# A planned attention order with waits, holds and 72 tries, and split weights at other addresses

## The chip, the cores and the metric

The kernel runs on one NeuronCore of one Trainium2 chip. TensorE (PE) does the matrix products and has a second row in the profile for the loading of its weights (PEld); VectorE (DVE), ScalarE (ACT) and GpSimd (POOL) do the elementwise work, and SyncE (SP) issues most transfers. SBUF has 128 partitions, which every engine addresses by bytes within a partition; PSUM has eight banks of 128 x 512 fp32. The metric is the device time of one execution in microseconds, as the median of several.

## The reference, cut to what matters

The input is 512 tokens of width 1024. There are two layers, all in fp32:

```python
for layer in range(2):
    sh1, sc1, g1, sh2, sc2, g2 = split(silu(c) @ ada_w[layer] + ada_b[layer], 6)
    u = rms_norm(h, norm_g[layer, 0]) * (1 + sc1) + sh1
    y = hgrn2_mixer(u, ...) if layer == 0 else dilated_attention_mixer(u, ...)
    h = h + (1 + g1) * rms_norm(y, norm_g[layer, 1])
    u = rms_norm(h, norm_g[layer, 2]) * (1 + sc2) + sh2
    gate, up = split(u @ ffn_w_in[layer], 2)          # 1024 -> 2 x 2816
    y = (silu(gate) * up) @ ffn_w_out[layer]          # 2816 -> 1024
    h = h + (1 + g2) * rms_norm(y, norm_g[layer, 3])
```

The attention mixer makes queries, keys and values for three groups of heads, eight heads of 128 each, with windows and dilations (128, 1), (512, 4) and (2048, 16). It rotates the first 32 channels of queries and keys, takes a softmax within each group's window, and weighs the three groups' outputs by a softmax over their log sums.

## The kernel before, in words

**Products.** An fp32 product is done as three passes of a faster type (fp32r): a number is cut into a high part (ACT copies it, `hi`) and the rest (DVE subtracts, `lo`), and `hi*hi + hi*lo + lo*hi` is summed in PSUM. Larger products are also done by a scheme with seven block products in place of eight; its blocks are 256 columns wide, so a seven-product unit has 7 x 12 = 84 matmuls of 256 columns.

**Weights.** `Stream` holds all weight loads in one list, `items`. Each is loaded by SP into one of two buffers `raw` (1 MB, tag "raw", `bufs=2`), in the order of the list. When an item has been worked off, its buffer takes the next load. Kinds of items: a weight (`"w"`) is cut into `hi` and `lo` (L89 and L90); a weight for seven products (`"quarters"`, `"half"`) is summed and cut by the stage itself; `"ada"` is 1 MB of `ada_w`, worked off by four DVE operations of 128 x 512 (L390 and L392, in attention L1931 and L1933), of which two items make one half of a modulation vector, summed over the partitions by POOL (`partition_all_reduce`, L394 and L1936); `"rows"` are two loads of 256 KB that finish half a gate (L439 and L440) after that sum; `"do"` finishes a shift or scale and loads nothing. `hi` and `lo` lie in a ring of three tiles of 2048 + 128 elements, that is 8704 bytes a partition, and `places(i, first)` takes 2048 elements of it from element `first` on. `first` is `R0` = 16 in the FFN, `V0[...]` for the four units of attention's values, `Q0[head]` for queries and keys. One element is 4 bytes.

**Where the modulation items lie.** `weave` puts them between the weights. In FFN 0, the first half of the weights (`f0a`) has three plain pairs of weights and then 16 quarters; the second half (`f0b`) has 11 weights of `ffn_w_out`. The gate of that layer (0, 5) needs four `ada` items (`gate_loads`) and two `rows` items (`gate_fins`); before, half of them lie among the plain weights of `f0a` and the rest in `f0b`, in front of the eight `ada` items of the next layer's shift and scale (`rest`). A group of `f0b` is placed after every 0.8 weights.

**The seven products of the FFN** (`seven_products`, PE's line is L958) work through 16 units in FFN 0 and 18 in FFN 1. A unit has three products that use the weight's own parts R (of `places(i)[0]`, cut by L921 and L925) and four that use its sums. POOL adds once per unit (L929), which gives a unit's period in the trace.

**Attention.** `Plan` gets the tasks of the attention stage with an engine, a cost and what they read and write. `run` gives each a due time, backwards from the place that a PE task has in the order of the program (`goal`), and then plays the engines forward: a free engine takes the ready task that is due first; the engines' programs are written out in that order, and each engine works in order. A task that follows on another engine is ready `late` after its predecessor's end (0.55 us after PE, 0.3 after a DMA, 0.08 otherwise, and 2.2 after the small transfers of POOL), on the same engine at once. An engine is left idle only for a task marked `urgent` that is about to be ready. `ticks` spreads a head's steps over the units of the following heads: scores at its begin + 3, 5 and 7 ticks, `merged` (the softmax over the groups) at + 9, the transposes of the probabilities (`flipped`, PE's line is L2313) at + 10 and + 11, the sums over values at + 11 and + 12. The last head's steps fall into the output projection (L577 to L579 there), which ticks seven times more. PE's line for the products of queries, keys and values is L1974. Attention's `ada` items lie in the plan too, with four POOL sums.

Of the kernel before, what the change touches and what calls it, by code (L numbers as in the profile page):

```python
# [2 lines left out]

# [7 lines left out]
F32 = mybir.dt.float32  # L11
# [5 lines left out]
P = 128  # L17
S = 512
D = 1024
# [16 lines left out]
R0, V0, Q0 = 16, (112, 96, 64, 16), (16, 16, 16, 16, 48, 80, 112, 0)  # L36
# [103 lines left out]
class Plan:  # L140


    LATE = {"PE": 0.55, "DMA": 0.3}

# [3 lines left out]
    def add(self, eng, cost, fn=None, r=(), w=(), goal=None, late=None, urgent=False, other=None):  # L148

        t = dict(id=len(self.tasks), eng=eng, cost=cost, fn=fn, goal=goal, urgent=urgent, other=other,  # L150
                 late=self.LATE.get(eng, 0.08) if late is None else late, deps=set(), outs=[])
# [33 lines left out]

    def run(self):

        ts = self.tasks
        for t in ts:
            for d in t["deps"]:  # L190
                ts[d]["outs"].append(t["id"])
        for t in reversed(ts):
            due = min([ts[o]["due"] - t["late"] for o in t["outs"]], default=1e9)
            if t["goal"] is not None:
                due = min(due, t["goal"] + t["cost"])
            t["due"] = due - t["cost"]
        left = {t["id"]: len(t["deps"]) for t in ts}
        ready, free, wait, done, now = {}, {}, {}, [], 0.0
        events = []

        def finish(t, at):
            for o in t["outs"]:
                u = ts[o]
                late = 0.0 if u["eng"] == t["eng"] else t["late"]
                ready[o] = max(ready.get(o, 0.0), at + late)
                left[o] -= 1
                if not left[o]:
                    enter(u)
                    heapq.heappush(events, ready[o])

        def enter(t):
            wait.setdefault(t["eng"], []).append(t["id"])
            if t["other"]:
                wait.setdefault(t["other"][0], []).append(t["id"])

        for t in ts:
            if not left[t["id"]]:
                ready[t["id"]] = 0.0
                enter(t)
        heapq.heappush(events, 0.0)  # L220
        while events:
            now = heapq.heappop(events)
            moved = True
            while moved:
                moved = False
                for eng in list(wait):
                    able = [i for i in wait[eng] if ready[i] <= now + 1e-9]
                    if not able or free.get(eng, 0.0) > now + 1e-9:
                        continue
                    able.sort(key=lambda i: (ts[i]["due"], i))  # L230
                    for i in able:
                        soon = [u for u in wait[eng] if now + 1e-9 < ready[u] < now + ts[i]["cost"] - 0.15 and ts[u]["urgent"]
                                and ts[u]["due"] < ts[i]["due"] + 3.0]
                        if eng is None or not soon or ts[i]["urgent"]:
                            break
                    else:
                        continue
                    t = ts[i]
                    wait[t["eng"]].remove(i)
                    if t["other"]:  # L240
                        wait[t["other"][0]].remove(i)
                        if eng != t["eng"]:
                            t["eng"], t["cost"] = t["other"]
                    t["start"] = now
# [4 lines left out]
                    finish(t, now + t["cost"])  # L249
                    moved = True  # L250
        assert len(done) == len(ts)
        for t in done:
            if t["fn"]:
                t["fn"](t["eng"])
        return done
# [36 lines left out]
def block_kernel(tc, x, c, positions, ada_w, ada_b, norm_g, hgrn_w_in, lower, hgrn_norm_g, hgrn_w_out,  # L292
# [8 lines left out]
    with ExitStack() as ctx:  # L301
# [580 lines left out]
        def seven_products(fs, mid, seeded, spare, th, tl):  # L882
# [34 lines left out]

            def r_hi(i):
                if i < len(fs):
                    raw[i] = st.whole()  # L920
                    act.copy(places(i)[0][0][:, 0:1536], raw[i][:, 512:])  # L921

            def r_lo(i):
                hi, lo = places(i)[0]
                dve.tensor_sub(lo[:, 0:1536], raw[i][:, 512:], hi[:, 0:1536].bitcast(F32))  # L925
# [43 lines left out]
            with tc.manual_schedule(engines=ORDERED):  # L969
# [950 lines left out]
        def condition(item):  # L1920
# [19 lines left out]
            if kind == "do":  # L1940
                col = ("col", (l, v, hf))
                for k in range(4):
                    c = l * 4 + v - (1 if v > 2 else 0)
                    DVE(0.36, lambda k=k: to_col(cols[:, c, hf * 4 + k:hf * 4 + k + 1], a.t, k), [a()], [col + (k,)])
# [7 lines left out]
            DVE(0.65, lambda: dve.tensor_add(half_of(), a.t, raw.t[:, 0:512]), [a(), raw()], [place(hf)])  # L1952
            DVE(0.7, lambda: dve.scalar_tensor_tensor(half_of(), half_of(), 1.0, raw.t[:, 512:D], op0=OP.add, op1=OP.mult),
# [29 lines left out]
        def turned(g, rows, q, k, last=False):  # L1983
# [3 lines left out]
            DVE(0.37, lambda: dve.stream_shuffle(rot.t, rows.t, [(i + 16) % 32 for i in range(32)]), [rows(i) for i in range(4)], [rot()])  # L1987
            DVE(0.36, lambda: dve.tensor_mul(rot.t, rot.t, cs[:, 1]), w=[rot()])
            DVE(0.36, lambda: dve.tensor_mul(rows.t, rows.t, cs[:, 0]), w=[rows(i) for i in range(4)])
            DVE(0.36, lambda: dve.tensor_add(rows.t, rows.t, rot.t), [rot()], [rows(i) for i in range(4)])  # L1990
# [7 lines left out]
            for i, t in enumerate((q, k)):  # L1998
                for hf in range(2):
# [6 lines left out]
                    ACT(0.38 if g else 0.62, back_to, [rows(2 * i + hf)], [t(hf)] if g else [t(0), t(1)])  # L2006
# [8 lines left out]
        def sevens(g, hd):  # L2015
            s_ = {}

            def cut(part, k):
                raw, p = s_["raw"], s_["p1"]
                ACT(0.58, lambda: act.copy(Q(p.t[0], part), Q(raw.t, k)), [raw(k)], [p("h", part)])  # L2020
                DVE(0.62, lambda: dve.tensor_sub(Q(p.t[1], part), Q(raw.t, k), Q(p.t[0], part).bitcast(F32)), [raw(k), p("h", part)], [p("l", part)])

            def add(to, k):
                raw = s_["raw"]
                DVE(0.62, lambda: dve.tensor_add(Q(raw.t, to), Q(raw.t, to), Q(raw.t, k)), [raw(k)], [raw(to)])
# [13 lines left out]
            def prepare_2():  # L2039
                raw = s_["raw"]  # L2040
                s_["p2"] = p = split_place(Q0[hd])
                for n in (1, 0):
                    two = slice(n * 1024, n * 1024 + 1024)
                    keys = [2 * n, 2 * n + 1]
                    ACT(1.0, lambda two=two: act.copy(p.t[0][:, two], raw.t[:, two]), [raw(k) for k in keys], [p("h", k) for k in keys])
                    DVE(1.15, lambda two=two: dve.tensor_sub(p.t[1][:, two], raw.t[:, two], p.t[0][:, two].bitcast(F32)),  # L2046
# [446 lines left out]
```

## Time and profile before

| | us |
|---|---|
| median of 3 runs | 1519.95 (1515.9 to 1520.64) |
| the profiled execution | 1517.82 |
| its span | 1516.1 |
| PE busy | 1487.4 (98%) |
| PEld busy | 1329.4 (88%) |
| DVE busy | 1100.0 (73%) |
| ACT busy | 797.3 (53%) |
| POOL busy | 199.9 (13%) |

Busy times are sums over the span, and matmuls overlap in them. Five stretches of the program matter below: FFN 0 with its seven products (from about 381 to 529 us of the span), its second half (to about 650), attention and its output projection (about 707 to 1155), FFN 1 with its seven products (from about 1201 to 1390), and its second half. PEclk is the share of full clock that PE was granted; it is 1 but for stretches of 3.4 us at 0.5. A row of the view by windows has, after the stretch and its length, each engine's busy time with its number of instructions, PEclk, the DMA engines' busy share and GB/s.

### The profile page before, as it was taken

Reading aid. Unit: us, or ns where it says so; the run is one execution under the profiler, and the core shown is the slowest. Engines: PE = TensorE matmul, PEld = TensorE weight load, DVE = VectorE, ACT = ScalarE, POOL = GpSimd, SP = SyncE. Lnnn points to the kernel's source line nnn. Section 1 sums busy time; section 2 is a strip of 40 time slices with the busy share of each in tenths; the row PEclk is TensorE's granted clock in tenths of the full one; section 3 lists DMA queues with packets and bytes.
Section 4 is the critical chain, followed back from the end, with each engine's and each line's share of the span. In section 5 each row is a group of like instructions: output and inputs, shape, how many; then the busy total and the mean of one; then the engine's idle time right before and its main releaser. Section 6 shows DMA issues by size and latency. Waiting matters only on the chain. (4 is left out here: it accounts for less than half of the span.)

```text
span 1516.1 us, 25045 instructions
## 1 busy us (share of the span) xinstructions
PE 1487.4 (98%) x9807; PEld 1329.4 (88%) x9807; DVE 1100.0 (73%) x1812; ACT 797.3 (53%) x1470; POOL 199.9 (13%) x174
## 2 busy tenths in 40 slices
PE   8999999999999999999999999999999999999998
PEld 6777888888999987888999989998978899999886
DVE  4587867587788776677888786778666967777633
ACT  4443434362555533375647787377875555555231
POOL 1011211031111101140001010001012211110100
PEclk9999999999999999999999999999999999999999
DMA  9654444225333356623254342434353323334531
GB/s 308 185 162 144 151 137 167 84 84 178 102 112 110 112 174 222 223 108 118 84 166 124 105 120 83 142 84 132 94 150 107 112 85 112 112 112 139 193 113 56
DMA packets 210151, 201.09 MB, mean 133 GB/s; under 512 B 8248, under 2 KB 167920, under 8 KB 209776
## 3 DMA queue, kind: packets, MB, share of 16 engines
q1 hardware_dynamic: 207056, 192.71, 40.8%
q10 hardware_dynamic: 1952, 6.65, 1.3%
q8 instruction: 77, 1.26, 0.3%
q0 software_dynamic: 1024, 0.13, 0.2%
q14 instruction: 42, 0.34, 0.1%
HBM read 192.31 MB, written 5.31 MB: 130 GB/s over the span
## 5 line engine op out<-in xcount | busy, mean ns | idle before, releaser
L89 ACT CAST hi<-raw 128x2048 fp32r<-128x2048 f32 x43 | 82.1, 1910 | 148.2 <-DMA raw<-in_ffn_w_out_dram 63.6
L90 DVE TENSOR_TENSOR lo<-raw,hi 128x2048 fp32r<-128x2048 f32 x43 | 102.8, 2392 | 60.7 <-ACT hi L89 60.6
L577 PE MATMUL ps_mm<-uh,hi 128*128 128x512 f32 (+1 forms) x400 | 145.8, 364 | 0.0
L578 PE MATMUL ps_mm<-ul,hi 128*128 128x512 f32 (+1 forms) x400 | 143.7, 359 | 1.1 <-DVE ul L677 1.1
L1974 PE MATMUL ps_mm<-apart,hiq 128*128 128x256 f32 (+1 forms) x608 | 144.7, 330 | 0.0
L579 PE MATMUL ps_mm<-uh,lo 128*128 128x512 f32 (+1 forms) x400 | 144.1, 360 | 0.2 <-DVE lo L90 0.2
L1974 PEld LDWEIGHTS ps_mm<-apart,hiq 128*128 128x128 f32 x608 | 100.7, 190 | 8.7
L1974 PE MATMUL ps_mm<-apart,loq 128*128 128x256 f32 (+1 forms) x304 | 98.7, 325 | 2.9 <-DVE loq L2046 2.9
L958 PE MATMUL ps_mm<-th,hiq 128*128 128x256 f32 x340 | 95.2, 280 | 0.0
L958 PE MATMUL ps_mm<-tl,hiq 128*128 128x256 f32 x340 | 95.1, 280 | 0.0
L958 PE MATMUL ps_mm<-th,loq 128*128 128x256 f32 x340 | 95.0, 279 | 0.0
L949 DVE TENSOR_TENSOR loq<-raw,hiq 128x1024 fp32r<-128x1024 f32 x68 | 80.3, 1221 | 17.1 <-ACT hiq L945 17.1
L577 PEld LDWEIGHTS ps_mm<-uh,hi 128*128 128x128 f32 x400 | 75.1, 188 | 19.7 <-issue 8.4
L578 PEld LDWEIGHTS ps_mm<-ul,hi 128*128 128x128 f32 x400 | 75.3, 188 | 12.2 <-DVE ul L677 1.5
L579 PEld LDWEIGHTS ps_mm<-uh,lo 128*128 128x128 f32 x400 | 75.1, 188 | 11.9 <-DVE lo L90 0.6
L929 POOL TENSOR_TENSOR raw<-raw 128x512 f32<-128x512 f32 x34 | 44.9, 1320 | 301.4 <-DVE loq L925 137.1
L577 PE MATMUL ps_mm<-hi,oh 128*128 128x512 f32 x208 | 81.4, 392 | 1.0 <-ACT hi L89 1.0
L578 PE MATMUL ps_mm<-lo,oh 128*128 128x512 f32 x208 | 81.2, 390 | 0.4 <-DVE lo L90 0.4
L945 ACT CAST hiq<-raw 128x1024 fp32r<-128x1024 f32 x68 | 68.1, 1047 | 17.3 <-DVE raw L933 15.6
L1974 PE MATMUL ps_mm<-uh,hiq 128*128 128x256 f32 x256 | 72.4, 283 | 1.9 <-DVE so L2245 1.1
L1974 PE MATMUL ps_mm<-uh,loq 128*128 128x256 f32 x256 | 71.6, 280 | 0.1
L1974 PE MATMUL ps_mm<-ul,hiq 128*128 128x256 f32 x256 | 71.6, 280 | 0.0
(477 smaller groups left out, 4650.8 us busy)
## 6 DMA issues: line engine op xcount, KB each, us to landing
raw<-in_ada_w_dram SPq DMA_DIRECT2D x40, 1024.0 KB, 5.2
raw<-in_ffn_w_in_dram SPq DMA_DIRECT2D x136, 256.0 KB, 3.8
raw<-in_ffn_w_out_dram SPq DMA_DIRECT2D x22, 1024.0 KB, 4.9
raw<-in_attn_w_in_dram SPq DMA_DIRECT2D x64, 256.0 KB, 4.6
raw<-in_hgrn_w_in_dram SPq DMA_DIRECT2D x12, 1024.0 KB, 5.3
raw<-in_attn_w_in_dram SPq DMA_DIRECT2D x12, 1024.0 KB, 5.1
raw<-in_ffn_w_in_dram SPq DMA_DIRECT2D x10, 1024.0 KB, 5.1
raw<-in_attn_w_in_dram SPq DMA_DIRECT2D x16, 512.0 KB, 5.2
```

The source lines that it names most:

```text
L89: self.nc.scalar.copy(hi, t)
L90: self.nc.vector.tensor_sub(lo, t, hi.bitcast(F32))
L577: pe.matmul(ps, ah, bh, start=start, stop=False, skip_group_check=part)
L578: pe.matmul(ps, ah, bl, start=False, stop=False, skip_group_check=part)
L579: pe.matmul(ps, al, bh, start=False, stop=stop, skip_group_check=part)
L929: pool.tensor_add(r[:, 2], r[:, 2], r[:, 0])
L945: act.copy(hi, src)
L949: dve.tensor_sub(lo, src, hi.bitcast(F32))
L958: pe.matmul(ps, w[x][:, a], us[kt][y], start=begin and kt + m == 0, stop=kt == 3 and m == 2, skip_group_check=True)
L1974: pe.matmul(dst(), x, y, start=begin and i == 0, stop=i == len(todo) - 1, skip_group_check=True)
```

## The change

Four things change.

1. **The planner.** A task that follows on the same DVE or ACT is ready 0.12 us after its predecessor (`DRAIN`), and `late` elsewhere is 0.18 instead of 0.08. A free engine may be held idle for any task that is due sooner (`better`). The whole play (`trial`) is run with 72 settings of the hold's four limits, and the order with the earliest modelled end of PE is kept. Costs of the ACT and DVE tasks are set anew by a few hundredths of a us (the small DVE tasks from 0.2 to 0.12).
2. **Ticks.** A head's transposes and sums come one tick later (+ 11, + 12, + 12, + 13), and the output projection ticks eight times, at other places.
3. **Places.** `V0` and `Q0` have other offsets, multiples of 4, 8, 16 or 32 bytes among them. In the FFN, the parts R of unit 1 alone lie 112 elements further, so at element 16 + 112 = 128 of their tile.
4. **FFN 0's modulation items.** All four `gate_loads` and both `gate_fins` lie in `f0b`, with a group after every 0.72 weights.

```diff
-R0, V0, Q0 = 16, (112, 96, 64, 16), (16, 16, 16, 16, 48, 80, 112, 0)
+R0, V0, Q0 = 16, (8, 24, 20, 64), (16, 24, 8, 20, 18, 17, 40, 80)
...
     LATE = {"PE": 0.55, "DMA": 0.3}
+    DRAIN = {"DVE": 0.12, "ACT": 0.12}
...
-                 late=self.LATE.get(eng, 0.08) if late is None else late, deps=set(), outs=[])
+                 late=self.LATE.get(eng, 0.18) if late is None else late, deps=set(), outs=[])
...
+    def after(self, t, u):
+        return self.DRAIN.get(t["eng"], 0.0) if u["eng"] == t["eng"] else t["late"]
+
+    def trial(self, due, sooner, least, ahead, price):
...
+        def better(i, u, now):
+            if not now + 1e-9 < ready[u] < 1e8 or due[u] > now + ahead:
+                return False
+            first = due[u] < due[i] - sooner or (ts[u]["urgent"] and not ts[i]["urgent"] and due[u] < due[i] + 3.0)
+            return first and now + ts[i]["cost"] - ready[u] > least + (ready[u] - now) * price
...
+                    able = sorted((i for i in wait[eng] if ready[i] <= now + 1e-9), key=lambda i: (due[i], i))
+                    pick = next((i for i in able if eng is None or not any(better(i, u, now) for u in wait[eng])), None)
...
+        return max(start[t["id"]] + t["cost"] for t in ts if t["eng"] == "PE"), done, start
...
+        tries = (self.trial(due, *rule) for rule in itertools.product((1, 2, 3, 5), (0.1, 0.2, 0.3), (5.0, 8.0, 1e9), (0.3, 1.0)))
+        end, done, start = min(tries, key=lambda r: r[0])
...
-        items += weave(f0a[:n0], [shift[3][1:], shift[5] + gate_loads[0], gate_loads[1], gate_fins[:1]], 2) + f0a[n0:]
-        gate = gate_loads[2:]
+        items += weave(f0a[:n0], [shift[3][1:], shift[5]], 2) + f0a[n0:]
         rest = ada_seq((1, 1), (1, 0))
-        items += weave(f0b, gate + [gate_fins[1:] + rest[0]] + rest[1:], 0, 0.8)
+        items += weave(f0b, gate_loads[:3] + [gate_fins[:1] + gate_loads[3], gate_fins[1:] + rest[0]] + rest[1:], 0, 0.72)
...
+            def rest(i):
+                o = 112 if i == 1 else 0
+                return [t[:, o:o + 1536] for t in places(i)[0]]
...
-                act.copy(places(i)[0][0][:, 0:1536], raw[i][:, 512:])
+                act.copy(rest(i)[0], raw[i][:, 512:])
...
-                    R, Sm = places(i)
+                    R, Sm = rest(i), places(i)[1]
...
-            ticks.add(n + 10, lambda: [flipped(i, f"p{k + 1}", "PR", range(4), k) for k in range(2)])
-            ticks.add(n + 11, lambda: sums_r(i))
-            ticks.add(n + 11, lambda: [flipped(i, "p0", "PN", range(1, 4), 0), flipped(i, "pn", "PN", range(4), 1)])
-            ticks.add(n + 12, lambda: sums_n(i))
+            ticks.add(n + 11, lambda: [flipped(i, f"p{k + 1}", "PR", range(4), k) for k in range(2)])
+            ticks.add(n + 12, lambda: sums_r(i))
+            ticks.add(n + 12, lambda: [flipped(i, "p0", "PN", range(1, 4), 0), flipped(i, "pn", "PN", range(4), 1)])
+            ticks.add(n + 13, lambda: sums_n(i))
...
-            for _ in range({0: 3, 2: 1, 4: 1, 5: 1, 6: 1}.get(kt, 0)):
+            for _ in range({0: 3, 1: 1, 2: 1, 3: 1, 5: 1, 6: 1}.get(kt, 0)):
```

More of the change, by code (lines that the diff above doesn't have):

```diff
@@ L2 @@
 import heapq
+import itertools
 import numpy as np
@@ L184, in place @@
         return Place(base, box)
-    def run(self):
+    def after(self, t, u):
+        return self.DRAIN.get(t["eng"], 0.0) if u["eng"] == t["eng"] else t["late"]
+    def trial(self, due, sooner, least, ahead, price):
         ts = self.tasks
[L189 to L214, printed above, removed]
+        left = [len(t["deps"]) for t in ts]
+        ready, free, wait, done, start = [0.0] * len(ts), {}, {}, [], {}
         for t in ts:
             if not left[t["id"]]:
-                ready[t["id"]] = 0.0
-                enter(t)
-        heapq.heappush(events, 0.0)
+                wait.setdefault(t["eng"], []).append(t["id"])
+        def better(i, u, now):
[3 more added lines that the diff above has]
+            return first and now + ts[i]["cost"] - ready[u] > least + (ready[u] - now) * price
+        events = [0.0]
         while events:
@@ L226, in run @@
                 for eng in list(wait):
-                    able = [i for i in wait[eng] if ready[i] <= now + 1e-9]
-                    if not able or free.get(eng, 0.0) > now + 1e-9:
+                    if free.get(eng, 0.0) > now + 1e-9:
                         continue
[L230 to L236, printed above, removed]
-                        continue
[L238 to L244, printed above, removed]
+                    able = sorted((i for i in wait[eng] if ready[i] <= now + 1e-9), key=lambda i: (due[i], i))
+                    pick = next((i for i in able if eng is None or not any(better(i, u, now) for u in wait[eng])), None)
+                    if pick is None:
+                        continue
+                    t = ts[pick]
+                    wait[eng].remove(pick)
+                    start[pick] = now
                     done.append(t)
@@ L2005, in back_to @@
                             act.copy(L4(dst)[:, 2 * hf:2 * hf + 2], src.rearrange("p (r l) -> p r l", r=2))
-                    ACT(0.38 if g else 0.62, back_to, [rows(2 * i + hf)], [t(hf)] if g else [t(0), t(1)])
+                    ACT(0.33 if g else 0.58, back_to, [rows(2 * i + hf)], [t(hf)] if g else [t(0), t(1)])
         def new_rows():
```

120 lines of the change are left out of this document (69 added, 51 removed).

## The prediction

> **What bounds the kernel now.** I read the page's busy times first.
>
> ```profile
> span 1516.1 us, 25045 instructions
> ...
> PE 1487.4 (98%) x9807; PEld 1329.4 (88%) x9807; DVE 1100.0 (73%) x1812; ACT 797.3 (53%) x1470; POOL 199.9 (13%) x174
> ```
>
> PE is busy for 98%, so it is the bound, and the change takes no matmul away. Only three things can be won or lost: PE's idle time, matmuls at half clock, and matmuls that take longer than others of the same size. The second view is a table of windows that puts the first two to their places (stretch, length, busy time and number of instructions of PE, PEld, DVE, ACT and POOL, granted clock, DMA share, GB/s).
>
> ```profile
> 380.00:400.00 20.00, 17.89 (x135) 17.25 (x134) 15.93 (x16) 9.94 (x15) 3.13 (x3) 0.91 0.37 106
> 400.00:520.00 120.00, 120.00 (x1062) 120.00 (x1061) 98.01 (x101) 70.46 (x114) 15.52 (x12) 1.00 0.38 107
> 537.80:641.00 103.20, 101.82 (x448) 83.15 (x447) 73.96 (x128) 32.95 (x35) 16.55 (x5) 1.00 0.63 210
> 705.00:1155.00 450.00, 439.70 (x3127) 410.55 (x3126) 343.71 (x740) 306.85 (x653) 36.21 (x39) 0.98 0.40 117
> 805.00:812.00 7.00, 6.65 (x54) 6.04 (x54) 6.68 (x20) 5.31 (x13) 3.12 (x1) 1.00 0.22 61
> 845.00:850.00 5.00, 4.22 (x36) 4.02 (x36) 4.86 (x17) 4.83 (x12) 0.00 (x0) 1.00 0.01 2
> 887.00:897.00 10.00, 7.87 (x55) 7.67 (x54) 7.51 (x16) 6.20 (x17) 3.23 (x1) 0.83 0.69 194
> 970.00:979.00 9.00, 6.94 (x46) 6.75 (x45) 7.85 (x10) 2.87 (x4) 0.00 (x0) 0.81 0.60 174
> 1049.00:1059.00 10.00, 7.95 (x64) 7.33 (x63) 7.66 (x25) 7.30 (x17) 0.34 (x1) 1.00 0.05 9
> 1122.00:1135.00 13.00, 10.16 (x45) 7.82 (x45) 9.81 (x23) 8.05 (x16) 3.23 (x1) 0.74 0.29 94
> 1215.00:1385.00 170.00, 170.00 (x1445) 170.00 (x1445) 130.96 (x134) 96.09 (x155) 20.68 (x16) 1.00 0.37 106
> ```
>
> Length less busy time is the idle time; length times the clock's lack of 1 is the clock's loss. At 380 that is 2.11 + 20 x 0.09 = 3.9 us, at 887 2.13 + 1.7 = 3.8, at 970 2.06 + 1.7 = 3.8, at 1122 2.84 + 3.4 = 6.2. Attention (705 to 1155) has 10.3 us idle, and the clock losses of those three windows are 6.8: 17.1 in all.
>
> The same rows show the third. FFN 0's seven products (400 to 520) and FFN 1's (1215 to 1385) have no gap and full clock, yet a matmul of 256 columns takes 120.00/1061 = 113.1 ns in the first and 170.00/1444 = 117.7 in the second (one less for the two cut by the ends). POOL, which adds once per unit, gives the periods:
>
> ```profile
> 406.73 1.29 POOL L929 TENSOR_TENSOR raw<-raw 128x512 f32<-128x512 f32 x1 [8.19 <-DVE loq L925]
> ...
> 520.97 1.29 POOL L929 TENSOR_TENSOR raw<-raw 128x512 f32<-128x512 f32 x1 [8.22 <-DVE loq L925]
> ...
> 1223.84 1.29 POOL L929 TENSOR_TENSOR raw<-raw 128x512 f32<-128x512 f32 x1 [14.03 <-DVE spare L925]
> ...
> 1372.24 1.29 POOL L929 TENSOR_TENSOR raw<-raw 128x512 f32<-128x512 f32 x1 [8.60 <-DVE loq L925]
> ```
>
> 12 periods of 9.52 us against 15 of 9.893, by the same lines at the same places. What differs is what stood in front: FFN 0 had the stall at 380, FFN 1 came out of running matmuls. Attention's four value units (L1974 alone: PE's busy time and number, clock, DMA share, GB/s) differ by their place, `V0` 112, 64, 96 and 16 in turn:
>
> ```profile
> 735.50:748.50 13.00, 13.00 (x117) 1.00 0.52 173
> 757.80:766.20 8.40, 8.40 (x72) 1.00 0.75 222
> 951.00:959.00 8.00, 8.00 (x70) 1.00 0.73 236
> 963.80:970.20 6.40, 6.40 (x59) 1.00 0.00 0
> ```
>
> With two taken off each count for the cut ones: 113.0, 120.0, 117.6 and 112.3 ns. Elements 64 and 96 are multiples of 128 bytes and are slow; 16 and 112 are 64 bytes off and fast, the last right behind a slow unit with no wait between. I take it that a place 64 off can run at either speed, keeps the one it is in, and is set to the fast one by a stall or by a stretch at a multiple of 128.
>
> **The change part by part.**
>
> *FFN 0's entry.* The raw buffers were held by two gate loads and one `rows`, and SP issued the first quarter late:
>
> ```profile
> 370.61 139.86 SPq L60 DMA_DIRECT2D raw<-in_ffn_w_in_dram  x64
> ```
>
> ```profile
> 375.91 1.48 ACT L921 CAST spare<-raw 128x1536 fp32r<-128x1536 f32 x1 [8.35 <-DMA raw<-in_ffn_w_in_dram]
> ```
>
> ACT waited 8.35 us there. Two gate loads and the rows leave this stage (their eight DVE operations, one POOL sum and SP's issues with them), and at 5.28 and 4.8 us each (worked out below) that is 15 us of loading in front of the quarters, more than ACT's wait. So the 3.9 us go. Next in line is nothing, since PE is then fed by the plain weights. But with the stall gone unit 0 runs slow, 84 x 4.6 ns = +0.4, and the 36 products with R of unit 1, now at element 128, take 120.0: 36 x 6.9 = +0.2. Net -3.3; the ends are 0 (another transfer is late instead) and -3.9.
>
> *FFN 1's unit 1.* It lies at 128 elements, 512 bytes, for its parts R. By the reading above that sets the speed: units 2 to 17, 16 x (9.893 - 9.52) = -6.0. The ends are 0 and -6.7 (all 18). I take -6.0 since the value units show the same step without a stall.
>
> *FFN 0's second half* gets what the first gave up: four `ada` and two `rows` items stand in front of w4 where two and one stood in front of w3. ACT's cutting of the weights shows what items cost:
>
> ```profile
> 554.66 1.92 ACT L89 CAST hi<-raw 128x2048 fp32r<-128x2048 f32 x1 [1.60 <-DMA raw<-in_ffn_w_out_dram]
> ...
> 568.58 1.91 ACT L89 CAST hi<-raw 128x2048 fp32r<-128x2048 f32 x1 [8.31 <-DMA raw<-in_ffn_w_out_dram]
> ...
> 577.70 1.91 ACT L89 CAST hi<-raw 128x2048 fp32r<-128x2048 f32 x1 [6.18 <-DMA raw<-in_ffn_w_out_dram]
> ...
> 592.10 1.90 ACT L89 CAST hi<-raw 128x2048 fp32r<-128x2048 f32 x1 [9.44 <-DMA raw<-in_ffn_w_out_dram]
> ```
>
> ```profile
> 570.55 0.49 PE L577 MATMUL ps_mm<-hi,oh 128*128 128x512 f32 x1
> ```
>
> These are w2 to w5, and each waited for its transfer. A step with one `ada` takes 9.12, with two 14.40, so an `ada` costs 5.28; one `ada` and one `rows` took 13.92, so `rows` cost 4.8. PE needs a weight every 48 x 101.82/448 = 10.9 us. After the change the order is w2, `ada`, w3, then `rows`, `ada`, `rows`, `ada`, then w4. So w3 is cut at 554.66 + 9.12 = 563.8, and w4 at 563.8 + 9.12 + 5.28 + 2 x 4.8 = 587.8, ready at 589.7. PE takes w3 at 570.0 (0.5 sooner than the row, as w3 was the late one) and wants w4 at 580.9: a stall of 8.8. That is beyond any cover, since DVE and ACT hold nothing else of the weights. The 1.4 us that this stretch idles now go (103.20 - 101.82), and a stall brings a half clock of 1.7 (as at 970): +9. Behind w4 come single and double `ada` steps in turn, 9.1 and 14.4 against 10.9 and 10.9, which give and take the same. The ends are 0 (the loads queue behind one another so that `rows` hide) and +12, if the second `rows` also holds its buffer through the POOL sum of 3.2 that it needs.
>
> *Attention's places.* `V0[3]` goes from 16 to 64: 84 x 7 ns = +0.6. Head 7's `Q0` goes from 0, a multiple of 128 bytes, to 80: 84 x 7 = -0.6. The other places are 4 to 32 bytes off, which no row shows. The ends are 113 and 120 ns for about 1,500 matmuls; they now stand 3.5 above 113 on average, 6.9 us over 1,986 in all, so +-5. I take 0.
>
> *The planner.* Its aim is the 17.1 us. What made them, by the rows of the engines at two of those places:
>
> ```profile
> 887.34 3.30 DVE L2046 TENSOR_TENSOR loq<-raw,hiq 128x1024 fp32r<-128x1024 f32 x1
> ...
> 891.25 1.21 DVE L2046 TENSOR_TENSOR loq<-raw,hiq 128x1024 fp32r<-128x1024 f32 x1
> ```
>
> ```profile
> 887.32 3.23 POOL L1936 PARTITION_ALL_REDUCE shared<-shared  x1 [7.88 <-DVE shared L1933]
> ```
>
> ```profile
> 1123.57 0.17 DVE L2290 TENSOR_TENSOR wM<-so 128x8 f32<-128x8 f32 x1 [5.08 <-DMA so<-scr]
> ```
>
> At 887 one DVE operation took 3.30 in place of 1.21, just as long as POOL's sum ran. The plan knows no such collision, so this 3.8 may go or come back anywhere. At 1122 the last head's `merged` waited 5.08 for a small transfer whose 2.2 the plan knew before; the tick for the transposes comes later, which hides a part. At 845, 970 and 1049 DVE and ACT follow their own results, which is what `DRAIN` describes: 0.8 + 3.8 + 2.05 = 6.6 are in its reach. I take all of that and 3 of the tail's 6.2, less 2 for half a new collision: -7.6. The ends are -14 (887 and the tail go whole: 3.8 and 3 more) and +6 (nothing cured, two small stalls new).
>
> Where a page speaks to that: the Trainium skill, SBUF — State Buffer, section "SBUF: two separate sides", has it that a VectorE operation with two SBUF inputs and a GpSimd operation that reads SBUF share a port pair as an exclusive lock. The trace agrees at 887 (3.30 against 1.21).
>
> *Sum:* -3.3 - 6.0 + 9.0 + 0 - 7.6 = -7.9 on the profiled execution's 1517.8, so 1509.9. The median of the runs is 2.1 above that execution: 1512.
>
> **The rivals.**
>
> *The second half doesn't stall.* If the two buffers let `rows` and `ada` run beside each other, w4 isn't late, and the sum is -16.9: 1503. For it: `rows` carry little data, and 4.8 is from one place only. Against it: all four weights above waited for their own transfers.
>
> *The kick does nothing.* Then only stalls make fast. FFN 1 stays at 9.893 (+6.0), and FFN 0, which has lost its stall, may run at it too: 15 more units, +5.6. That is 1518 to 1524. For it: both FFNs' rows differ by the stall alone. Against it: 963.8.
>
> Beside this stands the Trainium skill, TensorE: Matmul & The Clock Gate, section "Step-by-step: what each phase is for": loading the next weights goes through a read port of its own and takes nothing from the running matmul. By that rule places would be worth nothing. The periods of 9.52 and 9.893 with one code speak against it, and 120.0 against 113.0 too.
>
> *On the other side: POOL's sums meet DVE work that PE waits for.* Four sums of 3.2 lie in attention, at places that the new order moves; a hit costs 3.8 (887). If the plan cures nothing, the sum without it is -0.3, and from two hits more than now it is slower: +7.3, 1527. The plan cannot see them, and a new order draws all four anew, with DVE busy 343.71 of 450.
>
> *Attention's small offsets are slow:* +5, so 1517.
>
> **How the numbers follow.** 0.3% of 1520 is 4.6 us, about what a measurement of this kernel tells from no change; faster is below 1515.4, slower above 1524.5. Chances: the forecast (1512, own range 1504 to 1515) 0.40; no stall in the second half (1503) 0.24; the kick does nothing 0.12; the collisions (1527) 0.17; slow offsets (1517) 0.07. Faster is 0.40 + 0.24 = 0.64. Same is 0.07 + 0.09 of the kick's = 0.16. Slower is 0.17 + 0.03 = 0.20. The range is 1499 to 1527: below lies a planner at its -14 with no stall, above three hits.
>
> **What would show it.** Entry: no idle PE from 375 to 400, and ACT's first L921 some 10 us ahead of where it was. Kick: POOL's L929 in FFN 1 at 9.89 for two units and then 9.52, in FFN 0 9.5 after unit 1. Second half: one PE gap of about 9 before w4, behind an L89 that waits over 15 for its transfer. Planner: the windows' idle sum in attention down from 10.3 to about 5, with 970 and 1049 filled. I am wrong if L89 before w4 waits less than 12, if L929 stays at 9.89, or if a DVE operation of 3.3 in attention stands before idle PE at more places than now.

## The result, and the profile after

The changed kernel is slower: 1537.34 us median (1534.06 to 1538.52) beside 1517.93 for the kernel before in the same comparison, a ratio of 1.0129 with a 95% interval of 1.0094 to 1.0163. The forecast was 1512 with 1499 to 1527, so the time lies above the range. Two executions at a much lower clock (2678.93 us in the run `before, transfers at 4.4`, and 2463.67 us of the kernel before beside the joined runs) are left out of the ratios below. The page's head lines of the profiled execution (1538.52, the span 1536.8):

```profile
span 1536.8 us, 25032 instructions
...
PE 1497.7 (97%) x9807; PEld 1339.4 (87%) x9807; DVE 1095.0 (71%) x1812; ACT 798.2 (52%) x1470; POOL 198.6 (13%) x174
```

PE is busy 10.3 us longer and idle 10.4 us longer. To see where, I cut both traces at the same five matmuls: the first of FFN 0's seven products, the last of them, the first of attention, the first of FFN 1's seven products, the last of them. The view by windows (stretch, length, each engine's busy time and count, PEclk, DMA share, GB/s), first the kernel before, then the changed one:

```profile
381.22:538.05 156.83, 154.72 (x1346) 154.31 (x1345) 125.51 (x133) 89.22 (x146) 19.52 (x16) 0.99 0.39 115
538.05:707.34 169.29, 167.91 (x752) 137.92 (x752) 123.98 (x201) 76.82 (x115) 34.05 (x26) 1.00 0.52 172
707.34:1200.90 493.56, 481.87 (x3417) 449.13 (x3416) 382.62 (x793) 335.42 (x705) 51.42 (x51) 0.99 0.39 116
1200.90:1390.12 189.22, 189.22 (x1562) 187.25 (x1562) 143.99 (x150) 101.60 (x164) 21.98 (x17) 1.00 0.36 107
```

```profile
383.31:541.84 158.53, 158.53 (x1346) 158.53 (x1345) 118.37 (x125) 87.36 (x143) 18.29 (x15) 1.00 0.37 108
541.84:723.35 181.51, 169.38 (x753) 138.89 (x752) 132.87 (x211) 76.78 (x115) 36.78 (x27) 0.98 0.53 175
723.35:1221.60 498.25, 484.49 (x3418) 451.66 (x3417) 375.00 (x793) 335.22 (x705) 51.58 (x51) 0.99 0.38 115
1221.60:1410.84 189.24, 189.24 (x1562) 187.31 (x1561) 143.97 (x150) 101.60 (x164) 22.02 (x17) 1.00 0.36 107
```

| stage | before | after | difference | forecast |
|---|---|---|---|---|
| ahead of FFN 0's seven products | 381.2 | 383.3 | +2.1 | 0 |
| FFN 0's seven products | 156.8 | 158.5 | +1.7 | -3.3 |
| FFN 0's second half, on to attention | 169.3 | 181.5 | +12.2 | +9.0 |
| attention, on to FFN 1 | 493.6 | 498.2 | +4.7 | -7.6 |
| FFN 1's seven products | 189.2 | 189.2 | 0 | -6.0 |
| the rest | 126.0 | 126.0 | 0 | 0 |

The first row varies by itself: that stretch took 380.3 to 383.2 in the runs below, with the old order of items there and with the new one.

**The FFNs.** POOL's one operation per unit, changed kernel:

```profile
405.24 1.30 POOL L933 TENSOR_TENSOR raw<-raw 128x512 f32<-128x512 f32 x1 [8.68 <-DVE loq L929]
...
523.96 1.29 POOL L933 TENSOR_TENSOR raw<-raw 128x512 f32<-128x512 f32 x1 [8.59 <-DVE loq L929]
...
1254.45 1.30 POOL L933 TENSOR_TENSOR raw<-raw 128x512 f32<-128x512 f32 x1 [8.68 <-DVE loq L929]
...
1392.96 1.29 POOL L933 TENSOR_TENSOR raw<-raw 128x512 f32<-128x512 f32 x1 [8.59 <-DVE loq L929]
```

118.72/12 and 138.51/14 are both 9.893 us. The entry stall of FFN 0 is gone (158.53 of 158.53 busy), but both FFNs now run at the slow period from end to end.

**The second half.** ACT's cutting of w3 and w4, and PE's view of the waits:

```profile
567.32 1.91 ACT L90 CAST hi<-raw 128x2048 fp32r<-128x2048 f32 x1 [5.04 <-DMA raw<-in_ffn_w_out_dram]
...
591.19 1.90 ACT L90 CAST hi<-raw 128x2048 fp32r<-128x2048 f32 x1 [5.38 <-DMA raw<-in_ffn_w_out_dram]
```

```profile
PE ps_mm L577 <- ACT hi L90: 7.8, 1, 7.8
PE ps_mm L578 <- DVE lo L91: 2.6, 2, 1.4
```

The step is 23.87 us and PE waited 7.8 for its end. The 2.6 below it lie at the end of the stage, in front of the last weights. ACT's own wait before w4 is 5.38 only, since it did three other copies (`oh`, 574 to 586) in that step. The prediction had set a wait under 12 there as a sign of being wrong; the sign was badly chosen, for the step itself came out.

**Attention.** The largest stall lies at 828 to 832. In order of time: POOL's two small transfers of a head, DVE's first operation of `merged`, and ACT's:

```profile
822.53 0.54 POOL L2283 DMA_DIRECT2D scr<-so  x1 [58.03 <-ACT ps_mm L2067]
828.68 0.76 POOL L2285 DMA_DIRECT2D so<-scr  x1 [5.61 <-DMA scr<-so]
```

```profile
831.06 0.17 DVE L2294 TENSOR_TENSOR wM<-so 128x8 f32<-128x8 f32 x1 [4.93 <-DMA so<-scr]
```

```profile
831.47 0.21 ACT L2296 ACTIVATE wE<-wE 128x16 f32<-128x16 f32 x1 [4.53 <-DVE wE L2295]
```

```profile
826.00:836.00 10.00, 6.62 (x43) 6.42 (x42) 3.63 (x12) 5.47 (x15) 1.40 (x2) 0.77 0.36 95
```

The first transfer took until 828.68 and the second until 831.06: 8.5 us for the pair, where the plan has 0.6 + 2.2 + 0.75 + 2.2 = 5.75. DVE stood for 4.93 in front of `wM`, ACT behind it for 4.53 in front of `wE`, and PE, which needed ACT's next copies, lost 3.4 idle and, in that window, 10 x 0.23 = 2.3 to the half clock that followed. Over the whole stage, DVE's waits for `so<-scr` before `wM` (total, times, longest), before and after:

```profile
DVE wM L2290 <- DMA so<-scr: 12.7, 7, 5.1
```

```profile
DVE wM L2294 <- DMA so<-scr: 24.5, 8, 4.9
```

The rival that POOL's sums hit DVE more often is not what happened: of attention's DVE operations, two took over 2.5 us beside a sum in the kernel before (3.30 at 887, 2.88 at 1034) and one in the changed kernel (2.73 at 836).

### The profile page after: what moved, and what is told of

It is laid out like the page before. It is cut to its first block, busy times and chain, and to the rows that moved or that the text cites. A ratio compares the mean times of both kernels' runs of the same rounds, so it can differ in the third digit from the quotient of the medians.

```text
span 1536.8 us, 25032 instructions
## 1 busy us (share of the span) xinstructions
PE 1497.7 (97%) x9807; PEld 1339.4 (87%) x9807; DVE 1095.0 (71%) x1812; ACT 798.2 (52%) x1470; POOL 198.6 (13%) x174
## 5 line engine op out<-in xcount | busy, mean ns | idle before, releaser
L573 ACT CAST oh<-mid 128x512 fp32r<-128x512 f32 x44 | 26.4, 620 | 90.1 <-PE ps_b L578 78.1
```

The source lines that it names most:

```text
L573: act.copy(hi, src)
```

## The experiments

Stage lengths of each run's profile in us, by the same cuts, and its ratio to the kernel before on the same chip. In that order of columns: ahead, FFN 0's products, its second half, attention, FFN 1's products.

| run | ahead | FFN 0 | second half | attention | FFN 1 | ratio (95%) |
|---|---|---|---|---|---|---|
| old items | 382.7 | 162.4 | 167.2 | 497.5 | 189.3 | 1.0098 (1.0083 to 1.0113) |
| old places | 383.2 | 158.5 | 179.7 | 496.5 | 189.3 | 1.0148 (1.0131 to 1.0165) |
| old planner | 380.3 | 158.5 | 181.7 | 491.0 | 189.3 | 1.0103 (1.0088 to 1.0119) |
| shift by 128 bytes | 381.9 | 158.5 | 181.0 | 497.7 | 189.2 | 1.0156 (1.0141 to 1.0171) |
| transfers at 4.4 | 380.6 | 158.5 | 179.8 | 479.7 | 189.3 | 1.0011 (0.9992 to 1.0031) |
| spread, stalls | 383.1 | 154.0 | 185.6 | 499.1 | 185.2 | 1.0096 (1.0063 to 1.0129) |
| before, stall in FFN 1 | 380.9 | 160.3 | 168.6 | 492.5 | 184.0 | 0.9964 (0.9944 to 0.9984) |
| before, transfers at 4.4 | 381.5 | 161.2 | 166.9 | 493.1 | 189.2 | 1.0016 (0.9997 to 1.0035) |
| joined | 381.5 | 155.9 | 166.9 | 477.0 | 184.0 | 0.9892 (0.9866 to 0.9918) |
| joined, new places | 381.1 | 154.2 | 166.9 | 479.9 | 184.0 | 0.9925 (0.9899 to 0.9952) |
| joined, transfers at 6.0 | 381.0 | 155.1 | 168.2 | 481.1 | 184.0 | 0.9916 (0.9894 to 0.9939) |
| joined, old ticks | 381.1 | 157.2 | 167.0 | 480.0 | 184.0 | 0.9895 (0.9871 to 0.9919) |
| joined, one behind | 380.3 | 154.0 | 182.9 | 476.9 | 184.0 | one execution: 1505.77 beside 1514.91 |
| joined, none behind | 382.9 | 154.0 | 178.8 | 477.5 | 184.0 | one execution: 1504.81 beside 1514.91 |

How much one profile can tell is in the same table. The same attention code took 497.5 to 499.1 us in the changed kernel and three runs (old items, shift, spread), 492.5 and 493.6 in two profiles, and 476.9 to 477.5 in three: a difference under 2 us there says little by itself. FFN 0's products with the old items and no shift took 154.2 to 161.2 in seven profiles of the same code; the run with a stall in FFN 1 shows why.

### Old items in the changed kernel

```diff
-        items += weave(f0a[:n0], [shift[3][1:], shift[5]], 2) + f0a[n0:]
+        items += weave(f0a[:n0], [shift[3][1:], shift[5] + gate_loads[0], gate_loads[1], gate_fins[:1]], 2) + f0a[n0:]
+        gate = gate_loads[2:]
...
-        items += weave(f0b, gate_loads[:3] + [gate_fins[:1] + gate_loads[3], gate_fins[1:] + rest[0]] + rest[1:], 0, 0.72)
+        items += weave(f0b, gate + [gate_fins[1:] + rest[0]] + rest[1:], 0, 0.8)
```

> The changed kernel with FFN 0's modulation items where they were before. Theory (the long stall is the order of the items, and FFN 0's slow matmuls are the price of its missing entry stall): the stall before w4 goes (-12.2), the entry stall comes back (+3.9) and with it FFN 0's unit period of 9.52 (-5.6), so about -13.9 against the changed kernel: 1523. Rival (FFN 0 is slow because unit 1 lies elsewhere): the period stays at 9.89, so -8.3: 1529.

1526.71 us. The second half fell by 14.3 us to 167.2, so the items make its stall. But FFN 0's products took 162.4: the entry stall is back and the fast period isn't. My theory for FFN 0 fell, and the rival held. POOL's rows at the first units:

```profile
388.94 1.27 POOL L934 TENSOR_TENSOR raw<-raw 128x512 f32<-128x512 f32 x1 [6.79 <-DVE loq L930]
398.62 1.30 POOL L934 TENSOR_TENSOR raw<-raw 128x512 f32<-128x512 f32 x1 [8.41 <-DVE spare L930]
408.49 1.30 POOL L934 TENSOR_TENSOR raw<-raw 128x512 f32<-128x512 f32 x1 [8.57 <-DVE loq L930]
...
527.21 1.29 POOL L934 TENSOR_TENSOR raw<-raw 128x512 f32<-128x512 f32 x1 [8.59 <-DVE loq L930]
```

Behind the stall the matmuls of unit 0 start 113 ns apart; from unit 1's first product at element 128 on it is 120, then 118 to the end: (527.21 - 408.49)/12 = 9.89 per unit. PE stood nowhere between, so the shift that I took to set the fast speed is what ended it here.

### Old places in the changed kernel

```diff
-R0, V0, Q0 = 16, (8, 24, 20, 64), (16, 24, 8, 20, 18, 17, 40, 80)
+R0, V0, Q0 = 16, (112, 96, 64, 16), (16, 16, 16, 16, 48, 80, 112, 0)
```

> The changed kernel with the old V0 and Q0. Theory (small offsets run at 118 to 119 ns, the old ones partly at 113): -2.2 in attention's 256-column matmuls, 1535; the stalls in attention about as in the changed kernel. Rival (places are worth nothing, what differs is the planner's order): 1537 and the same 256-column excess.

1534.34 us, attention 1.8 shorter. Summed over the 256-column products of queries, keys and values whose next one starts within 130 ns, the excess over 113.3 ns fell from 9.3 us to 6.6. The theory held: with the new places these products start 118.1 ns apart on average, with the old ones 116.7.

### The old planner with the rest of the change

The kernel before with the new `V0` and `Q0`, `rest(i)` and order of items; `Plan`, costs and ticks stay.

> The kernel before with the new places, the new unit 1 and the new order of FFN 0's items, but the old planner, ticks and costs. Theory (the planner's new order is worth nothing or a little less than the old one): idle and half-clock time in attention as before, so -2 to -3 against the changed kernel: 1535. Rival (the planner gained, and the new places took it): attention gets longer than in the changed kernel by 3 or more: 1540.

1527.96 us, attention 491.0: 7.2 shorter than in the changed kernel. The new order costs more than I had it: the theory's sign held, not its size. The old planner's attention is also 2.6 shorter than in the kernel before, although its 256-column excess rose from 7.0 us to 9.4; the stall at 970 of the kernel before had shrunk from 3.8 us to under 1. Why is not settled, and the old planner's attention took 492.5 in another profile, so a part of the 2.6 is noise.

### From unit 1 on, 128 bytes further

```diff
+            def turn(i):
+                return 32 if i >= 1 else 0
...
-                o = 112 if i == 1 else 0
-                return [t[:, o:o + 1536] for t in places(i)[0]]
+                o = turn(i)
+                if i % 2:
+                    return [t[:, o:o + 1536] for t in places(i)[0]]
+                return [spare[0][:, o:o + 1536], spare[1][:, 32 - o:32 - o + 1536]]
```

The sums move in the same way, and the tiles are 32 elements longer. In every second unit the low part moves by the same 128 bytes towards the front.

> The changed kernel, but from unit 1 on all parts of a unit lie 32 elements (128 bytes) further, in both FFNs, in place of unit 1's R alone 112 elements further. Theory (a matmul stream 64 off has two speeds, and a jump of one operand by 128 bytes changes the one into the other, as in attention where the moving operand jumps): the unit period goes from 9.89 to 9.52 in both FFNs from unit 1 or 2 on, 15 x 0.37 + 17 x 0.37 = -11.8: 1525.5. Rival (only a stall sets the speed): 9.89 in all units, 1537.

1534.99 us, and FFN 0's window shows no change of speed (158.45/1345 = 117.8 ns):

```profile
381.89:540.34 158.45, 158.45 (x1346) 158.45 (x1345) 118.30 (x125) 87.37 (x143) 18.24 (x15) 1.00 0.36 108
```

The theory fell. A jump of the stationary operand (the weight, which stays in the array while the other one streams past) by 128 bytes does not make a slow stream fast.

### POOL's transfers at 4.4 us in the new plan

```diff
-                     [("scr", hd, 0)], late=2.2)
+                     [("scr", hd, 0)], late=4.4)
```

The same at all four of them.

> The changed kernel with 4.4 us in place of 2.2 as the plan's time for each of POOL's four small transfers. Theory (the new plan puts the merge's first operation at the head of DVE's queue when a transfer should have come by its 2.2 us; it comes 4 to 5 us later, DVE stands, ACT stands behind it, and PE behind ACT): DVE's waits for so<-scr before wM of 4.9, 3.8, 4.5 and 4.9 us become under 1.5 each, and attention gets about 6 us shorter than the changed kernel's 498.2 (to the first product of FFN 1). Rival (a later merge only moves the wait to the transposes): the waits go, but PE waits there, and the stage stays within 2 of 498.

1517.09 us. DVE's waits before `wM`, and attention's window:

```profile
DVE wM L2294 <- DMA so<-scr: 4.2, 5, 2.2
```

```profile
718.95:1198.67 479.72, 476.51 (x3417) 445.96 (x3417) 374.73 (x793) 335.18 (x705) 51.78 (x51) 1.00 0.39 119
```

The waits fell from 24.5 to 4.2, and attention by 18.5 us, three times what I expected: 10.5 of it is idle time (13.8 to 3.2), and 8.0 is busy time, most of which half clock had stretched (PEclk 0.99 to 1.00). The new planner is good for 14 us against the kernel before, and one wrong cost hid it. The edit draws the whole order anew, so the run shows what the cost is worth in all, not wait by wait.

### Items spread, and stalls on purpose

```diff
+        g, (r0, r1), t = gate_loads, gate_fins, [i for k in rest for i in k]
+        groups = [g[0], g[1], g[2], [r0] + g[3], [r1], t[:2], t[2:4], t[4:5], t[5:7], t[7:8], t[8:]]
+        for i, w in enumerate(f0b):
+            items += [w] + groups[i]
...
+                        for _ in range({6: 3, 4: 4}[fs[0]] if i == 0 else 0):
+                            hi, lo, src = s_cut(1, 1)
+                            dve.tensor_sub(lo, src, hi.bitcast(F32))
                         s_lo(i + 1, 1)
```

`fs[0]` is 6 in FFN 0 and 4 in FFN 1; unit 1's shift is taken out.

> The changed kernel with three edits in three stages that don't touch each other. FFN 0's second half: the same modulation items, but never more than one rows and one ada, or two ada, between two weights. Theory (loads in front of w4 make its stall): the stage from FFN 0's seven products to attention falls from 181.5 to 170. Rival (the second rows waits for POOL's sum, and everything behind it): it stays above 178. The FFNs: unit 1's R back at its place, and DVE repeats one operation of 1.2 us three times in FFN 0 and four times in FFN 1 ahead of unit 1's sums, so PE should stand once for 0.7 and 1.9 us. Theory (a stall inside the stream sets the fast speed): FFN 0's products 158.5 to 154, FFN 1's 189.3 to 185. Rival (only a stall that also halves the clock does): 159 and 191. In all 1537 - 20 = 1517 by the theory.

1531.41 us. FFN 0's products took 154.0 and FFN 1's 185.2, so a short stall inside the stream can set the fast speed. In the second half the theory's 170 did not come, it took 185.6: the weights came in time but for one wait of 0.9 us, and a stall stood at the stage's end. A window up to 636, PE's wait there, and POOL:

```profile
537.10:636.00 98.90, 98.90 (x437) 81.66 (x437) 71.28 (x109) 29.54 (x32) 15.94 (x5) 1.00 0.61 206
```

```profile
PE ps_mm L661 <- DVE xn L655: 14.3, 3, 12.5
```

```profile
647.25 3.23 POOL L395 PARTITION_ALL_REDUCE shared<-shared  x1 [9.92 <-DVE shared L393]
657.93 0.59 POOL L631 TENSOR_TENSOR rr<-rv,expo 128x1 f32<-128x1 f32 x1 [7.45 <-issue]
```

The last sum ended at 650.48, and POOL did nothing for 7.45 us before the norm's small operation. Its input from DVE was there at 652.87; for the 5.06 us behind that the profile shows no wait.

### The kernel before with a stall in FFN 1

The same repeated operation, three times, in FFN 1 alone of the kernel before.

> The kernel before with the one repeated DVE operation, three times, in FFN 1 alone. Theory: PE stands 0.7 us in unit 1, and units 2 to 17 run at 9.52: FFN 1's products from 189.2 to 184, and the whole is 5 faster than before. Rival (the speed needs the half clock, or the stall is hidden): 189 to 190, no gain.

1509.09 us, 0.36% faster. PE's window around it, and POOL's rows:

```profile
1200.00:1240.00 40.00, 39.50 (x283) 36.78 (x282) 31.97 (x33) 18.05 (x29) 3.87 (x3) 1.00 0.28 80
```

```profile
1245.38 1.29 POOL L929 TENSOR_TENSOR raw<-raw 128x512 f32<-128x512 f32 x1 [8.31 <-DVE spare L925]
...
1369.14 1.29 POOL L929 TENSOR_TENSOR raw<-raw 128x512 f32<-128x512 f32 x1 [8.22 <-DVE loq L925]
```

0.5 us idle in two waits (0.3 and 0.2) at full clock, and 123.76/13 = 9.52 from then on. The theory held: neither a place nor the half clock is needed.

FFN 0 of the same run shows the other direction. Its code is that of the kernel before, its entry stall came (0.5 and 0.8 us in two waits) and made unit 0 fast. Then two matmuls came late by 0.25 us together (their starts lie 0.25 and 0.23 us apart in place of 0.113), and from there on it was slow, 118.72/12 = 9.89 per unit:

```profile
390.88 0.28 PE L958 MATMUL ps_mm<-th,spare 128*128 128x256 f32 x1
391.13 0.39 PE L958 MATMUL ps_mm<-uh,hiq 128*128 128x256 f32 x1
391.36 0.28 PE L958 MATMUL ps_mm<-ul,hiq 128*128 128x256 f32 x1
391.47 0.28 PE L958 MATMUL ps_mm<-uh,loq 128*128 128x256 f32 x1
```

```profile
404.61 1.29 POOL L929 TENSOR_TENSOR raw<-raw 128x512 f32<-128x512 f32 x1 [8.67 <-DVE loq L925]
...
523.33 1.29 POOL L929 TENSOR_TENSOR raw<-raw 128x512 f32<-128x512 f32 x1 [8.60 <-DVE loq L925]
```

The next run's FFN 0 fell in the same way at 392; the joined kernel's had the same two late starts at 393 and stayed fast. So an interruption sets the speed anew, and not always to the fast one: counted over PE's start times within both FFNs' seven products, in all sixteen profiles, 31 of 35 interruptions (starts over 0.14 us apart) left it fast and 4 slow. What decides is open.

### The kernel before with transfers at 4.4 us

The old plan with the edit of the run on transfers.

> The kernel before with 4.4 us in place of 2.2 for POOL's small transfers in the old plan. Theory (the time of the transfers is wrong in the old plan too, but its order hits the wait only at the last head, 5.08 us): attention 1 to 3 us shorter than 493.6. Rival (the old plan has no such fault, a new order draws new stalls): within 2 of 493.6 or longer.

1519.1 us, attention 493.1. DVE's waits before `wM` fell from 12.7 to 6.1, but PE's waits in attention moved to other places (12.0 us in all, 11.2 before). The rival held: the old planner gains nothing from the larger cost, the new one does.

### Joined

The changed kernel with old items, old places and no shift, with 4.4 us for the transfers, and with the stall in FFN 1 (three repeats).

> The new planner and its ticks with 4.4 us for POOL's small transfers, the old places, FFN 0's items as before, no shift of unit 1, and the repeated DVE operation in FFN 1. Theory: attention 479.7 less the 2.3 of the places = 477.4, FFN 0 and its second half together as in the kernel before (326 to 329, its products at 9.52 after the entry stall since unit 1's shift is gone), FFN 1's products 184: 16 + 5 shorter than the kernel before, 1.4% faster. Rival (the 18 us of the new plan hung on the places or on when the weights come): attention above 485, under 1% faster.

1494.52 us beside 1511.27, and attention as forecast from the parts:

```profile
704.26:1181.22 476.96, 473.73 (x3417) 442.77 (x3416) 374.86 (x793) 335.11 (x705) 51.99 (x51) 1.00 0.39 120
```

It beats both kernels. FFN 0, with the entry stall and without unit 1's shift, is fast in this profile (155.9); the same code was slow in the two before it.

### Joined, with one thing else

The new `V0` and `Q0`; 6.0 in place of 4.4; the old ticks.

> The same with the new V0 and Q0. Theory (small offsets cost 113 to 119 ns): 2.3 us longer in attention than with the old places. Rival (places are worth nothing under this order): the same within 1 us.

> The joined kernel with 6.0 us in place of 4.4 for POOL's small transfers. Theory (4.4 has some waits before wM left, 4.2 us in five): those go too, and attention is 0 to 2 us shorter. Rival (a merge planned that late pushes the transposes past their ticks): PE waits before the transposes and attention is 3 or more longer.

> The joined kernel with the old ticks (transposes and sums one tick sooner, seven ticks in the output projection). Theory (the later transposes are what leaves the merge time for its transfers): PE waits for ACT's h before the transposes, and attention is 5 or more longer. Rival (the order alone does it): within 2 us.

The new places cost 2.9 us of attention, as the theory had it. At 6.0 attention is 4.1 longer, as long as its rival had it, so 4.4 is not only a bound to stay above; PE's waits are spread over several places, the longest 0.9 us. The old ticks cost 3.1 in attention's profile, between theory and rival, with one wait of 1.5 us for ACT's `h` before the transposes, and the whole times (1494.5 and 1495.4) don't differ: most of the 16.6 is the order's, 3 us at most the ticks'.

### Joined, with the gate in the second half after all

```diff
-        groups = [g[0], g[1], g[2], [r0] + g[3], [r1], t[:2], t[2:4], t[4:5], t[5:7], t[7:8], t[8:]]
+        groups = [g[0], g[1], g[2], [r0] + g[3], [r1], t[:2], t[2:4], t[4:5], t[5:8], t[8:10], t[10:]]
```

and, for none behind, the last six groups are `t[:2]`, `t[2:4]`, `t[4:6]`, `t[6:9]`, `t[9:]` and an empty one.

> The joined kernel with FFN 0's gate items in its second half, spread as in the run before with spread items, but with one ada item behind the last weight in place of two, and the repeated DVE operation in FFN 0 too. Theory (the last POOL sum, which took 3.23 and was followed by 7.45 us in which POOL did nothing before the norm's operation, made the 12.5 us stall at the layer's end): the last sum lies 5 us sooner and the stage from FFN 0's products to attention falls from 185.6 to about 180. Rival (the stage is full of loads, whatever the order): 183 to 186.

> The same with no ada item behind the last weight. Theory: the last sum and the 7.45 us lie before the layer's end, what is left are some 3 us in front of the ninth weight, behind two ada items: the stage takes 170 to 173. Rival (full of loads): 178 or more, with the stall in front of the last weights instead.

182.9 and 178.8 us. The theory's 180 and 170 to 173 were too short, and the rival's 178 or more held. In the first run the stall at the layer's end shrank from 12.5 to 4.9; in the second it is gone, and the stall stands in front of the late weights again (4.0 and 3.4 us of waits for their parts). In all four orders tried the stage is 12 to 19 us longer than the 166.9 without the two `ada` and the `rows`, whose loads are 2 x 5.28 + 4.8 = 15.4. That it is full of loads fits this; that no order is shorter is not shown.

## Why the prediction was wrong, by its steps

The forecast sum was -7.9, the profiled spans differ by +20.7. The difference of 28.6 is attention 12.3, FFN 1 6.0, FFN 0 5.0, the second half 3.2, and 2.1 ahead of the change. Two steps failed: the rule for what sets the fast speed (11 us), and the price of the planner's new order (12.3 with the places).

*FFN 0's entry.* The stall went, as written. What failed is the reading that a stretch at a multiple of 128 bytes sets the fast speed, by which FFN 0 was taken as fast from unit 2 on. Only 0.4 + 0.2 us were put against the 3.9; it was the full 5.6 of the rival in which only stalls make fast. The prediction had that case, with its times 1518 to 1524, at 0.12. The choice went wrong at one row, the value unit at 963.8: there the moving operand came to a place 64 bytes off behind a stretch at a multiple of 128, while in the FFN the weight is the stationary one. That this is the difference is likely and not shown. The shift of 128 bytes showed that such a jump of the stationary side does not make fast, and old items showed the shift to a multiple of 128 ending the fast speed. The other half of the reading, that a stall makes fast, failed too, and the trace of the kernel before had the row. Behind the stall at 970 to 976 the same value unit went on at the same place:

```profile
976.60:982.80 6.20, 6.20 (x55) 6.20 (x55) 1.00 0.75 235
```

That is 6.20/53 = 117.0 ns, counted like the 112.3 at 963.8 in front of the stall: here a stall made a fast stream slow.

*FFN 1's unit 1.* -6.0 became 0, by the same error. The gain itself is there and was sized right: with a stall of 0.5 us FFN 1 is 5.2 shorter. The Trainium skill, TensorE: Matmul & The Clock Gate, section "Step-by-step: what each phase is for", has it that loading the next weights takes nothing from the running matmul. By that alone places would be worth nothing. Here the same 84 matmuls take 9.52 or 9.89 us by their place and by what went before, so the measurement stands against places being worth nothing.

*The second half.* The mechanism and the step held to 0.1 us (24.0 forecast, 23.87). What failed is "give and take the same" behind w4: PE stood 2.6 us more in front of the last weights and 1.7 more at the norm behind them, less the 1.0 by which the stall before w4 was shorter than forecast (7.8 for 8.8). The sum over the loads, 15.4, would have been nearer to the 12.2 than the one gap was.

*Attention's places.* Taken as 0 between -5 and +5; 2 to 3 us slower. Its two terms of 0.6 should be 1.2 each, since a value unit and a head's queries and keys have 168 such matmuls and not 84; they cancel all the same.

*The planner.* The headroom of 17.1 was right: the joined kernel's attention is 16.6 shorter. What failed is the step that priced the new order by which old stalls it cures. I named the 2.2 us of the small transfers, saw 5.08 at the last head, and took it for the tail's alone. In the changed kernel DVE waited for it at all eight heads: the pairs took 4.5 to 8.5 us, five of them more than the 5.75 planned. The same edit to 4.4 is worth 18.5 us under the new plan and 0.5 under the old one; that this is because the new plan packs DVE tighter is an argument, not shown. The rival on the slower side had the right form (the plan cannot see something), and the wrong thing, POOL's sums.

## What to carry to other kernels

Before an order by a planner is judged, compare the costs it assumes with the trace for every kind of task that another engine's queue stands behind; for the small transfers neither the usual time nor the longest was the best cost: of 2.2, 4.4 and 6.0 us the middle one gave the shortest attention, and they took from 2.1 to 7.25. When loads are moved between stages, add up all loads of the stage against its length before looking at gaps. Where two stretches of one code run at different speeds, change one thing of the history at a time: a stall that looks like a loss may be what makes the rest fast, or slow. And look at several profiles of the same code before a speed is put down to a cause.

## What the runs showed of the hardware

- A stream of 256-column matmuls with its parts 64 bytes off ran at 117.7 or at 113.2 ns each, and kept its speed for 18 units. PE stalls of 0.5 us together at full clock turned slow into fast (the stall in FFN 1). Two late starts, 0.25 us together, turned fast into slow (FFN 0 of that run), and so did the stall of 2.06 us at 970 in the kernel before and 12 products at a multiple of 128 bytes (old items).
- One small transfer through POOL's queue, from its issue to the next issue that waited for it, took from 2.1 us (1069.12 to 1071.22 in the changed kernel) to 7.25 (838.49 to 845.74).
- Behind a sum over the partitions, POOL's next elementwise operation began 7.45 us later, 5.06 us after its input was there (spread items); 7.00 us later, 3.2 after its input, in the run with one behind. No trace here has one sooner than 7.0.
- The half clock came behind single idle stretches of 2.13 and 2.06 us (887 and 970 in the kernel before) and of 1.8 (951 with old places), and not behind one of 3.2 (830 with the shift of 128 bytes). The 2.05 us idle at 1049, without half clock, were two waits of 1.1 and 0.8 and smaller ones. The Trainium skill, TensorE: Matmul & The Clock Gate, section "Why this matters for your kernels", warns of gaps over some 3 us; the traces have it from 1.8 us on, and not each time at 3.2.
